# The beginning of a 256-token, four-layer network on one core: the first norm's weights spread by transposes, the first tile's squares and scaling split over two engines

## Chip, cores and metric

The kernel runs on one core of a Trainium2 chip. The metric is the device time of one execution in microseconds; the figure of a kernel is the median of its runs. One execution is also recorded by the hardware profiler, and all times "from the span's start" below are from that record. The engines are TensorE (PE, with its weight loads PEld), VectorE (DVE), ScalarE (ACT), GpSimd (POOL) and SyncE (SP), which here only issues DMAs.

## What is computed

Four layers over x of shape (1, 256, 1024): stick-breaking attention with a gated convolution MLP, forgetting attention with another, a pooling layer and a latent attention layer. What matters here is the very first step, the RMS norm of x with the weights `sb_pre_g`, and the projection to values that follows it:

```python
def rmsnorm(x, g):
    xf = x.astype(jnp.float32)
    y = xf * lax.rsqrt(jnp.mean(xf * xf, axis=-1, keepdims=True) + RMS_EPS)
    return (y * g.astype(jnp.float32)).astype(x.dtype)
...
a = rmsnorm(h, sb_pre_g[layer])
q, k, v = jnp.split(a @ sb_w_qkv[layer], 3, axis=-1)
```

## The kernel before

**Tiling.** The 256 tokens are two tiles of 128 (i = 0 and 1), one token a partition; `h[:, i, :]` holds the 1024 features of a token. A norm works on that layout: the squares of a row are summed (`square`, ACT, two halves of 512 features, `HALF`), POOL makes the reciprocal root (`rstd_of`: two adds and a power), and `scaled` multiplies h by it and by the norm's weights on DVE, in two halves, into a tile `a`. The weights have to stand in all 128 partitions for this; `gain` (L301) loads them with a DMA that reads the same 4 KB row for each partition, 512 KB in all.

**Transposes.** The matmuls need features on the partitions. `transpose_split` (L341) lets TensorE transpose four 128x128 blocks of `a` into one PSUM tile `psT`, then splits the result into two fp32r numbers: `hi_copy` (L55, ACT) rounds it, `lo_sub` (L59, DVE) takes the rest. `aT[n]` holds features 512n to 512n+511; `all_T` does both n.

**Weights.** Each weight chunk is loaded into `raw` by SP (`load_w`, L141, ring of three), and split in parts the same way, `wh` on ACT and `wl` on DVE (`bg_hi`, `bg_lo`; `bg(m)` puts m parts into the engines' queues). The first two chunks come in eight parts of one block of 128 features by 512 columns each; with the sixth part's DMA the second token tile of x is loaded (L150). A product is three matmuls (L78, L79, L81): high by high, high by low, low by high.

**Order.** Nothing is scheduled by a planner: each engine works off its queue in the order in which the code is written, and waits by semaphores for the others. At the beginning (L565 to L584) that is: 24 transposes of the identity on TensorE into a tile `warm` that nobody reads, the norm of token tile 0 (`a0`), `bg(2)` for weight parts 0 and 1, `all_T(a0)`, `bg(4)`, the squares of tile 1, `bg(2)`, the scaling of tile 1 (`a1`), then `values_all`, whose first group of matmuls (n = 0, i = 0) reads `aT` of tile 0; `all_T(a1)` stands behind this group and ahead of the second one (n = 0, i = 1).

SP's queue at the beginning: both halves of tile 0 of x, the norm's weights, six weight parts, tile 1 of x, two more weight parts, and then whole chunks.

PSUM: two pools of four tiles (2 KB a partition), `pacc` (accumulators) and `pmm` (short-lived results).

Of the kernel before, what the change touches and what calls it, by code (L numbers as in the profile page):

```python
# [7 lines left out]
F32 = mybir.dt.float32  # L8
# [3 lines left out]
AF = mybir.ActivationFunctionType  # L12
ALU = mybir.AluOpType
PSUM = bass.MemoryType.PSUM

P = 128
S = 256
NT = S // P
D = 1024
KD = D // P  # L20
# [4 lines left out]
EPS = 1e-6  # L25
# [10 lines left out]
def tile_net(ctx: ExitStack, tc: tile.TileContext, t, out):  # L36
    nc = tc.nc
    ctx.enter_context(tc.manual_schedule())
    pe, act, dve, pool = nc.tensor, nc.scalar, nc.vector, nc.gpsimd
# [6 lines left out]
    nat = ctx.enter_context(tc.tile_pool(name="nat", bufs=2))  # L46
    jk = ctx.enter_context(tc.tile_pool(name="jk", bufs=1))
    sm = ctx.enter_context(tc.tile_pool(name="sm", bufs=4))
# [15 lines left out]
    def split(hi, lo, src, scale=None):  # L64

        hi_copy(hi, src, 1.0 if scale is None else scale)
        lo_sub(lo, src, hi, scale)
# [15 lines left out]
    def acc_tile(name):  # L83
        return pacc.tile([P, 512], F32, tag="acc", name=name)
# [4 lines left out]
    def mm_tile(name):  # L89
        return pmm.tile([P, 512], F32, tag="mm", name=name)  # L90

    def tok(i):
        return slice(i * P, (i + 1) * P)
# [11 lines left out]
    def table_set(i):  # L105
        act.add_instruction(mybir.InstLoadActFuncSet(
            act_func_set_id=i, name=nc.get_next_instruction_name()))
# [33 lines left out]
    def load_w(upto):  # L141
        while nxt["load"] <= min(upto, len(specs) - 1):
            v = specs[nxt["load"]][0]
            raw = rawp.tile([P, RAWW], F32, tag="raw", name="raw")
            rv = raw[:, :v.shape[1] * v.shape[2]].rearrange("p (a b) -> p a b", a=v.shape[1])

            for q in specs[nxt["load"]][1] if nxt["load"] < 2 else ():
                k0, k1 = parts[q]["cut"][0:2]
                nc.sync.dma_start(out=rv[:, k0:k1], in_=v[:, k0:k1])
                if q == 5:  # L150
                    load_x(1)
            if nxt["load"] >= 2:
                nc.sync.dma_start(out=rv, in_=v)
            loaded[nxt["load"]] = rv
            nxt["load"] += 1

    def bg_hi():

        n = nxt["hi"]
        if n >= len(parts) or (n >= WBUFS and parts[n - WBUFS]["used"] < parts[n - WBUFS]["need"]):  # L160
            return False
        q = parts[n]
        load_w(q["chunk"])
        k0, k1, c0, c1 = q["cut"]
        for nm, pl_ in (("wh", whp), ("wl", wlp)):
            w = pl_.tile([P, TW], F32R, tag=nm, name=nm)
            q[nm] = w[:, :q["n"]].rearrange("p (a b) -> p a b", a=k1 - k0)
        q["raw"] = loaded[q["chunk"]][:, k0:k1, c0:c1]
        hi_copy(q["wh"], q["raw"], q["scale"] or 1.0)
        nxt["hi"] += 1  # L170
        return True

    def bg_lo():
        while nxt["lo"] < nxt["hi"]:
            n = nxt["lo"]
            q = parts[n]
            lo_sub(q["wl"], q.pop("raw"), q["wh"], q["scale"])
            nxt["lo"] += 1
            if n == specs[q["chunk"]][1][-1]:
                load_w(q["chunk"] + RAWB)  # L180

    def bg(m=1):
        for _ in range(m):
            bg_lo()
            if not bg_hi():
                break
        bg_lo()
# [104 lines left out]
    h = cst.tile([P, NT, D], F32, name="h")  # L292

    def load_x(i):
        for n in range(2):
            s_ = slice(512 * n, 512 * n + 512)
            nc.sync.dma_start(out=h[:, i, s_], in_=t["x"][0, tok(i), s_])

    load_x(0)

    def gain(name, idx=None, g=None):  # L301
        src = t[name][idx] if idx is not None else t[name]
        n = src.shape[0]
        if g is None:
            g = gp.tile([P, D], F32, tag="g", name="g")[:, 0:n]
        nc.sync.dma_start(out=g, in_=src.unsqueeze(0).to_broadcast([P, n]))
        return g

    g_pre = gain("sb_pre_g", 0)
    load_w(RAWB - 1)  # L310


    ident = cst.tile([P, P], F32, name="ident")
# [3 lines left out]
    epsc = cst.tile([P, 2], F32, name="epsc")  # L317
# [7 lines left out]
    def mean_sq(srcs, n):  # L325

        ss = sm.tile([P, 2], F32, tag="ss", name="ss")
        for j, x in enumerate(srcs):
            square(x, n, ss[:, j:j + 1])
        return ss[:, 0:len(srcs)]  # L330

    def rstd_of(ss, tag="rstd"):
        r = sm.tile([P, 1], F32, tag=tag, name="rstd")
        s0 = ss[:, 0:1]
        pool.tensor_tensor(out=s0, in0=s0, in1=epsc[:, 0:1], op=ALU.add)  # L335
        if ss.shape[1] == 2:
            pool.tensor_tensor(out=s0, in0=s0, in1=ss[:, 1:2], op=ALU.add)
        pool.tensor_tensor(out=r, in0=s0, in1=epsc[:, 1:2], op=ALU.pow)
        return r

    def transpose_split(src, dst, i, b, m=4):  # L341

        ps = mm_tile("psT")
        for j in range(m):
            pe.transpose(ps[:, tok(j)], src[:, tok(b + j)], ident)  # L345
        split(dst[0][:, 0:m, tok(i)], dst[1][:, 0:m, tok(i)],
              ps[:, 0:m * P].rearrange("p (k c) -> p k c", k=m))

    def all_T(src, dst, i):
        for n in range(2):  # L350
            transpose_split(src, dst[n], i, 4 * n)

    HALF = [slice(n * 512, (n + 1) * 512) for n in range(2)]

    def scaled(i, r, g):

        a = nat.tile([P, D], F32, tag="a", name="a")
        for s_ in HALF:
            dve.scalar_tensor_tensor(out=a[:, s_], in0=h[:, i, s_], scalar=r, in1=g[:, s_],
                                     op0=ALU.mult, op1=ALU.mult)  # L360
        return a
# [7 lines left out]
    def square(x, n, ss):  # L369

        junk = jk.tile([P, 512], BF16, tag="junk", name="junk")
        act.activation(out=junk[:, 0:x.shape[1]], in_=x, func=AF.Square, scale=float(n) ** -0.5,  # L372
                       accum_out=ss)
# [28 lines left out]
    def new_aT():  # L402
        return [tuple(atp.tile([P, KD // 2, S], F32R, tag=f"aT{x}{n}", name="aT") for x in "hl")
                for n in range(2)]
# [62 lines left out]
    def edge(tail0, tail1, acc, add, g, dst):  # L467


        tail0()  # L470
        half, fin = add(0, acc[0])
        half(0)
        half(1)
        bg_hi()
        fin()
        r0 = norm_r(0)
        tail1()
        half, fin = add(1, acc[1])
        half(0)
        a0 = scaled(0, r0, g)  # L480
        half(1)
        all_T(a0, dst, 0)
        bg_hi()
        fin()
        r1 = norm_r(1)
        return scaled(1, r1, g), (r0, r1)
# [78 lines left out]
    K8 = [(k, k) for k in range(KD)]  # L565
    aT = new_aT()
    table_set(NLE_SET)
    warm = mm_tile("warm")
    for _ in range(24):
        pe.transpose(warm[:, 0:P], ident, ident)  # L570
    a0 = scaled(0, rstd_of(mean_sq([h[:, 0, s_] for s_ in HALF], D)), g_pre)
    bg(2)
    all_T(a0, aT, 0)
    bg(4)
    ss1 = mean_sq([h[:, 1, s_] for s_ in HALF], D)
    bg(2)
    a1 = scaled(1, rstd_of(ss1, "rn"), g_pre)
    bg(0)
    with tc.tile_pool(name="sb", bufs=2) as sb, tc.tile_pool(name="sbv", bufs=1) as sbv:
        vv = [sbv.tile([P, NT, D], F32R, name=n) for n in ("vh", "vl")]  # L580
# [95 lines left out]
        with tc.tile_pool(name="ld", bufs=1) as ld:  # L676
            a1 = attention(s0, s1, s2, s3, post, W["sb_o"], oT, g_post, aT2,
                           lambda: load_params(ld), lambda: gain("ffn_pre_g", 0), mm_tile)
        aT = aT2
# [113 lines left out]
    with tc.tile_pool(name="fxa", bufs=1) as fxa:  # L793
# [3 lines left out]
        a1, rn = ffn(0, aT, a1, lambda: (gain("ffn_post_g", 0), gain("kv_norm_g")), sT)  # L797
# [3 lines left out]
        with tc.tile_pool(name="fx", bufs=2) as fx, tc.tile_pool(name="fxv", bufs=1) as fxv:  # L801
# [26 lines left out]
            for b in (0, 32, 64, 96):  # L828
# [16 lines left out]
                                     op1=ALU.subtract)  # L845
            pool.memset(fe, 1.0)
            dve.tensor_tensor_scan(out=fc, data0=fe, data1=fy, initial=0.0, op0=ALU.mult,
                                   op1=ALU.add)
# [45 lines left out]
            def f3(p):  # L894
                heads_out(p, vv, st.pop(("p", p)), oT)

            aT = new_aT()
            a1 = attention(f0, f1, f2, f3, lambda p: bg(1), W["fx_o"], oT, g_post, aT,
                                     gates_T, lambda: gain("ffn_pre_g", 1), acc_tile)

    pT = new_aT()
    a1 = ffn(1, aT, a1, lambda: (gain("ffn_post_g", 1), gain("pool_norm_2", 0)), pT)[0]
    aT = pT


    with tc.tile_pool(name="pl", bufs=2) as pl_, tc.tile_pool(name="plc", bufs=1) as plc:
# [95 lines left out]
        g_pre = gain("mla_norm_2", 0)  # L1002
# [28 lines left out]
        def lat_mm(x, i, k0, k1):  # L1031
            n, w = lat_w[x]
            if k0 == 0:
# [5 lines left out]
        a1 = edge(lambda: out_rows(acc[0], 0, st["y", 3], wo, k4, False, True, by_half=True),  # L1039
                  lambda: out_rows(acc[1], 1, st["y", 3], wo, k4, False, True, by_half=True),  # L1040
                  acc, plain_add, g_pre, mT)[0]
        aT = mT
# [407 lines left out]
```

## Time and profile before

| | |
|---|---|
| median of 3 runs | 996.11 us (993.27, 996.11, 997.5) |
| profiled execution, its own time | 995.02 us |
| its span, first to last instruction | 992.6 us |
| mean granted TensorE clock | 0.997 |
| TensorE busy | 977.5 us (98%) |
| DVE, ACT, POOL busy | 754.3, 608.4, 72.4 us |
| DMA traffic over the span | 171 GB/s read |

A row of the timeline has the start and the length in us, the engine, the line of the kernel, the operation, what it writes and reads, a count where equal instructions were merged, and in brackets the idle time of the engine ahead of it with what ended it. The chain of waits is followed back from the last instruction: at each step to what released it. Rows that group instructions have busy us, mean ns of one, and the idle time ahead. A matmul's length contains the pipeline behind it, so that matmuls in a row overlap: their pace is read from the starts, or from the chain.

### The profile page before, as it was taken

To read this page: it belongs to the slowest core of one execution; us is meant where nothing else is said; L and a number is where in the kernel's file an instruction comes from. 1 tells how busy PE (TensorE), PEld (TensorE's weight loads), DVE (VectorE), ACT (ScalarE), POOL (GpSimd) and SP (SyncE) were. 2 spreads that over 40 slices of the span, in tenths; PEclk is the share of its full clock that TensorE was granted. 3 is DMA by queue.
4 is the path that set the end of the run, shared out by engine and by line. 5 is a ranking of instruction groups with operands and counts; after the bars stand their busy time and mean duration, and the time that the engine had idled before them with its cause. 6 is when DMAs were issued, how large, how long until landed. Compare 5 with 4: busy or idle time off the path is not lost.

```text
span 992.6 us, 17595 instructions
## 1 busy us (share of the span) xinstructions
PE 977.5 (98%) x6955; PEld 900.3 (91%) x6955; DVE 754.3 (76%) x1299; ACT 608.4 (61%) x1050; POOL 72.4 (7%) x182
## 2 busy tenths in 40 slices
PE   8999999999999999999999999999999999999997
PEld 6999789999887799879999988899999899999996
DVE  6577788899845879977999954777757677886876
ACT  6489867677634657666667643565535455766663
POOL 1022220000001100020000000200000020110100
PEclk9999999999999999999999999999999999999999
DMA  8824346575652654435665665275555344544421
GB/s 300 258 87 148 128 152 212 163 243 191 249 193 85 197 188 149 151 105 170 208 203 184 212 241 184 68 253 207 178 208 191 109 133 134 202 156 138 160 100 42
DMA packets 116292, 170.79 MB, mean 172 GB/s; under 512 B 4226, under 2 KB 93682, under 8 KB 116210
## 3 DMA queue, kind: packets, MB, share of 16 engines
q1 hardware_dynamic: 116146, 169.68, 51.6%
q8 instruction: 54, 0.88, 0.4%
q14 instruction: 28, 0.23, 0.1%
q0 software_dynamic: 64, 0.00, 0.0%
HBM read 168.62 MB, written 1.05 MB: 171 GB/s over the span
## 4 chain that ended last, share of the span: by engine, by line
PE 92%; DVE 3%; ACT 2%; DMA 1%; issue 1%; POOL 1%; SPq 0%; POOLq 0%; DVEq 0%; ACTq 0%
PE psu L70 10%; PE psu L71 10%; PE psu L72 10%; PE accD L71 4%; PE accD L72 4%; PE accD L70 4%; PE psq L70 4%; PE psq L72 4%; PE psq L71 4%; PE accO L70 3%; PE accO L72 3%; PE accO L71 2%; PE accP L71 2%; PE accP L72 2%; PE accP L70 2%; PE psT L345 1%
## 5 line engine op out<-in xcount | busy, mean ns | idle before, releaser
L59 DVE TENSOR_TENSOR wl<-raw,wh 128x1024 fp32r<-128x1024 f32 (+3 forms) x300 | 352.6, 1196 | 102.6 <-ACT wh L55 99.6
L55 ACT ACTIVATE wh<-raw 128x1024 fp32r<-128x1024 f32 (+3 forms) x316 | 315.5, 1026 | 98.9 <-PE accD L72 44.8
L70 PE MATMUL psu<-aT,wh 128*128 128x256 f32 x864 | 241.3, 279 | 0.0
L71 PE MATMUL psu<-aT,wh 128*128 128x256 f32 x864 | 240.6, 278 | 0.0
L72 PE MATMUL psu<-aT,wl 128*128 128x256 f32 x864 | 240.4, 278 | 0.0
L70 PEld LDWEIGHTS psu<-aT,wh 128*128 128x128 f32 x864 | 162.2, 188 | 0.0
L72 PEld LDWEIGHTS psu<-aT,wl 128*128 128x128 f32 x864 | 162.2, 188 | 0.0
L71 PEld LDWEIGHTS psu<-aT,wh 128*128 128x128 f32 x864 | 161.9, 187 | 0.0
L703 DVE SCALAR_TENSOR_TENSOR yc<-psu,conv,yc 128x255 f32<-128x255 f32 (+1 forms) x160 | 73.3, 479 | 7.7 <-ACT yc L696 4.7
L70 PE MATMUL accD<-wh,gh 128*128 128x512 f32 x176 | 69.3, 394 | 0.0
L71 PE MATMUL accD<-wl,gh 128*128 128x512 f32 x176 | 69.3, 394 | 0.0
L72 PE MATMUL accD<-wh,gl 128*128 128x512 f32 x176 | 69.3, 394 | 0.0
L335 POOL TENSOR_TENSOR ss<-ss,epsc 128x1 f32<-128x1 f32 x24 | 11.7, 488 | 625.5 <-ACT junk L372 625.4
L70 PE MATMUL psq<-aT,wh 128*128 128x256 f32 x192 | 54.1, 282 | 0.1
L72 PE MATMUL psq<-aT,wl 128*128 128x256 f32 x192 | 53.5, 279 | 0.0
L71 PE MATMUL psq<-aT,wh 128*128 128x256 f32 x192 | 53.5, 279 | 0.0
L708 ACT ACTIVATE yc<-yc 128x256 f32<-128x256 f32 x44 | 18.4, 418 | 54.2 <-DVE yc L703 54.2
L696 ACT ACTIVATE yc<-psu,conv 128x256 f32<-128x256 f32 x80 | 40.5, 556 | 8.2 <-PE psu L72 8.2
L72 PEld LDWEIGHTS accD<-wh,gl 128*128 128x128 f32 x176 | 32.9, 187 | 8.1
L70 PEld LDWEIGHTS accD<-wh,gh 128*128 128x128 f32 x176 | 32.9, 187 | 8.1
L71 PEld LDWEIGHTS accD<-wl,gh 128*128 128x128 f32 x176 | 32.9, 187 | 8.1
L55 ACT ACTIVATE qkh<-psq 128x512 fp32r<-128x512 f32 x32 | 19.0, 594 | 31.9 <-PE psq L72 31.6
(334 smaller groups left out, 2276.0 us busy)
## 6 DMA issues: line engine op xcount, KB each, us to landing
raw<-in_w_up_dram SPq DMA_DIRECT2D x44, 1024.0 KB, 5.1
raw<-in_w_down_dram SPq DMA_DIRECT2D x22, 1024.0 KB, 4.9
raw<-in_pool_w_in_dram SPq DMA_DIRECT2D x16, 1024.0 KB, 7.6
raw<-in_sb_w_qkv_dram SPq DMA_DIRECT2D x10, 1024.0 KB, 6.2
raw<-in_w_kvf_dram SPq DMA_DIRECT2D x8, 1024.0 KB, 5.6
raw<-in_pool_w_out_dram SPq DMA_DIRECT2D x8, 1024.0 KB, 5.2
raw<-in_mla_w_in_dram SPq DMA_DIRECT2D x8, 1024.0 KB, 5.5
raw<-in_mla_w_out_dram SPq DMA_DIRECT2D x8, 1024.0 KB, 6.4
```

Of the source, the lines that this page charges most:

```text
L55: act.activation(out=hi, in_=src, func=AF.Copy, scale=scale)
L59: (eng or dve).tensor_tensor(out=lo, in0=src, in1=hi.bitcast(F32), op=ALU.subtract)
L70: pe.matmul(ps, lhsT=l[0], rhs=r[0], start=first, stop=False)
L71: pe.matmul(ps, lhsT=l[0], rhs=r[1], start=False, stop=False)
L72: pe.matmul(ps, lhsT=l[1], rhs=r[0], start=False, stop=last)
L335: pool.tensor_tensor(out=s0, in0=s0, in1=epsc[:, 0:1], op=ALU.add)
L345: pe.transpose(ps[:, tok(j)], src[:, tok(b + j)], ident)
L696: act.activation(out=y[:, u, :], in_=ps[:, u * S:(u + 1) * S], func=AF.Identity, bias=cp[:, 132 + q:133 + q], scale=cp[:, 88 + q:89 + q])
L703: dve.scalar_tensor_tensor(out=y[:, u, d:S], in0=ps[:, u * S:(u + 1) * S - d], scalar=w, in1=y[:, u, d:S], op0=ALU.mult, op1=ALU.add)
L708: act.activation(out=y[:, 0, :], in_=y[:, 0, :], func=AF.Gelu_apprx_tanh)
```

## The change

1. `g_pre = gain(...)`, the 512 KB DMA on SP, is gone. Instead ACT issues, ahead of its table load, a DMA of the 1024 weights as 8 rows of 128 (`g_row`, 4 KB).
2. TensorE transposes `g_row` into PSUM (`gT_ps`), DVE copies the result to `g_col` (128 partitions, 8 columns), and TensorE transposes each column, repeated 128 times by a step of zero, into `g_ps`, two PSUM tiles of 128x512 in which each partition holds the weights. Blocks 4 to 7 come first. Around these stand 7, 3 and 4 transposes of the identity in place of the 24.
3. The squares of tile 0: ACT takes half 0, DVE half 1 (`tensor_tensor_reduce`, with the division by 1024 and EPS folded in; so POOL's add of EPS is gone).
4. The scaling of tile 0: half 0 in one DVE instruction as before; half 1 is multiplied by the weights on DVE (`y0`) ahead of the reciprocal root, and by that root on ACT.
5. Weight part 0 is split ahead of `aT[0]` and part 1 ahead of `aT[1]`, instead of both ahead of both.
6. Tile 1 is scaled by the weights out of PSUM.

```diff
+    g_row = sm.tile([KD, P], F32, tag="grow", name="g_row", bufs=1)
+    act.dma_start(out=g_row, in_=t["sb_pre_g"][0].rearrange("(k p) -> k p", p=P))
     load_x(0)
...
-    g_pre = gain("sb_pre_g", 0)
     load_w(RAWB - 1)
...
-    warm = mm_tile("warm")
-    for _ in range(24):
-        pe.transpose(warm[:, 0:P], ident, ident)
-    a0 = scaled(0, rstd_of(mean_sq([h[:, 0, s_] for s_ in HALF], D)), g_pre)
-    bg(2)
-    all_T(a0, aT, 0)
+    warm = acc_tile("warm")
+
+    def busy(n):
+        for _ in range(n):
+            pe.transpose(warm[:, 0:P], ident, ident)
+
+    busy(7)
+    gT_ps = acc_tile("gT_ps")
+    pe.transpose(gT_ps[:, 0:KD], g_row, ident[0:KD, 0:KD])
+    g_col = sm.tile([P, KD], F32, tag="gcol", name="g_col", bufs=1)
+    dve.tensor_copy(g_col, gT_ps[:, 0:KD])
+    busy(3)
+    g_ps = [mm_tile("g_ps") for n in range(2)]
+    for k in (4, 5, 6, 7, 0, 1, 2, 3):
+        pe.transpose(g_ps[k // 4][:, tok(k % 4)], g_col[:, k:k + 1].to_broadcast([P, P]), ident)
+    busy(4)
+
+    ss0 = sm.tile([P, 2], F32, tag="ss", name="ss")
+    square(h[:, 0, HALF[0]], D, ss0[:, 0:1])
+    a0 = nat.tile([P, D], F32, tag="a", name="a")
+    y0 = nat.tile([P, D], F32, tag="a", name="y0")
+    dve.tensor_tensor_reduce(out=y0[:, HALF[0]], in0=h[:, 0, HALF[1]], in1=h[:, 0, HALF[1]],
+                             scale=1.0 / D, scalar=EPS, op0=ALU.mult, op1=ALU.add,
+                             accum_out=ss0[:, 1:2])
+    dve.tensor_tensor(out=y0[:, HALF[1]], in0=h[:, 0, HALF[1]], in1=g_ps[1], op=ALU.mult)
+    r0 = sm.tile([P, 1], F32, tag="rstd", name="rstd")
+    pool.tensor_tensor(out=ss0[:, 0:1], in0=ss0[:, 0:1], in1=ss0[:, 1:2], op=ALU.add)
+    pool.tensor_tensor(out=r0, in0=ss0[:, 0:1], in1=epsc[:, 1:2], op=ALU.pow)
+    act.activation(out=a0[:, HALF[1]], in_=y0[:, HALF[1]], func=AF.Copy, scale=r0)
+    dve.scalar_tensor_tensor(out=a0[:, HALF[0]], in0=h[:, 0, HALF[0]], scalar=r0, in1=g_ps[0],
+                             op0=ALU.mult, op1=ALU.mult)
+    for n in range(2):
+        bg(1)
+        transpose_split(a0, aT[n], 0, 4 * n)
     bg(4)
     ss1 = mean_sq([h[:, 1, s_] for s_ in HALF], D)
     bg(2)
-    a1 = scaled(1, rstd_of(ss1, "rn"), g_pre)
+    r1 = rstd_of(ss1, "rn")
+    a1 = nat.tile([P, D], F32, tag="a", name="a")
+    for n, s_ in enumerate(HALF):
+        dve.scalar_tensor_tensor(out=a1[:, s_], in0=h[:, 1, s_], scalar=r1, in1=g_ps[n],
+                                 op0=ALU.mult, op1=ALU.mult)
```

The order on ACT from the start of the program to the last part of the first two chunks: before,

```order
L106 ACT_TABLE_LOAD
L372 ACTIVATE junk,ss<-h 128x512 x2
L55 ACTIVATE wh<-raw 128x512 x2
L55 ACTIVATE aT<-psT 128x4x128 x2
L55 ACTIVATE wh<-raw 128x512 x4
L372 ACTIVATE junk,ss<-h 128x512 x2
L55 ACTIVATE wh<-raw 128x512 x2
```

and now (line numbers are those of the changed kernel):

```order
L301 DMA g_row<-in_sb_pre_g_dram 8x128
L106 ACT_TABLE_LOAD
L374 ACTIVATE junk,ss<-h 128x512
L598 ACTIVATE a<-y_160,rstd 128x512
L55 ACTIVATE wh<-raw 128x512
L55 ACTIVATE aT<-psT 128x4x128
L55 ACTIVATE wh<-raw 128x512
L55 ACTIVATE aT<-psT 128x4x128
L55 ACTIVATE wh<-raw 128x512 x4
L374 ACTIVATE junk,ss<-h 128x512 x2
L55 ACTIVATE wh<-raw 128x512 x2
```

One of the two squares of tile 0 has gone to DVE, half of the scaling has come in its place, and the first two parts and the two halves of `aT` alternate.

On DVE, the same place of the program, as a difference (ISA is the multiply with a sum, and the read of that sum):

```order
-L359 SCALAR_TENSOR_TENSOR a<-h,rstd,g 128x512 x2
-L59 TENSOR_TENSOR wl<-raw,wh 128x512 x2
-L59 TENSOR_TENSOR aT<-psT,aT 128x4x128 x2
+L1480 UNCONDITIONAL_BRANCH
+L580 COPY g_col<-gT_ps 128x8
+L591 ISA y_160,ss<-h 128x512
+L591 ISA ss 128x1
+L594 TENSOR_TENSOR y_160<-h,g_ps 128x512
+L599 SCALAR_TENSOR_TENSOR a<-h,rstd,g_ps 128x512
+L59 TENSOR_TENSOR wl<-raw,wh 128x512
+L59 TENSOR_TENSOR aT<-psT,aT 128x4x128
```

DVE had nothing to do ahead of the scaling; now a copy that waits for TensorE, a square and a multiply stand there, and one half of the scaling is left.

On TensorE, ahead of the first matmul with weights:

```order
-L570 MATMUL warm<-ident 128x128 x24
-L345 MATMUL psT<-ident,a 128x128 x8
+L1480 UNCONDITIONAL_BRANCH
+L574 MATMUL warm<-ident 128x128 x7
+L578 MATMUL gT_ps<-ident,g_row 128x8
+L574 MATMUL warm<-ident 128x128 x3
+L584 MATMUL g_ps<-ident,g_col 128x128 x8
+L574 MATMUL warm<-ident 128x128 x4
+L347 MATMUL psT<-ident,a 128x128 x8
```

The transposes for the weights stand between those of the identity, the first behind a DMA and the eight behind DVE's copy.

On SP one row is gone, the DMA of the norm's weights between x and the first weight part; all its other rows stand in the order of before.

## The prediction

> **What bounds the kernel now.** I read the page first, then the span in two stretches, then the chain of waits and the timeline of the first 18 us.
>
> The page: the span, TensorE's share, and the shares of the chain that ended last.
>
> ```profile
> span 992.6 us, 17595 instructions
> PE 977.5 (98%) x6955; PEld 900.3 (91%) x6955; DVE 754.3 (76%) x1299; ACT 608.4 (61%) x1050; POOL 72.4 (7%) x182
> ...
> PE 92%; DVE 3%; ACT 2%; DMA 1%; issue 1%; POOL 1%; SPq 0%; POOLq 0%; DVEq 0%; ACTq 0%
> ```
>
> Two stretches, cut where the second group of value matmuls starts (stretch, length, busy time of PE, PEld, DVE, ACT and POOL with counts, granted clock, DMA share, GB/s).
>
> ```profile
> 0.00:18.10 18.10, 14.16 (x64) 11.24 (x64) 8.98 (x14) 10.13 (x20) 3.07 (x15) 0.91 0.89 317
> 18.10:992.60 974.50, 963.37 (x6891) 889.04 (x6891) 745.32 (x1285) 598.29 (x1030) 69.29 (x167) 1.00 0.51 169
> ```
>
> Behind 18.1 us TensorE works 963.4 of 974.5 us, and the change touches nothing there. Ahead of it 3.9 us are idle, and much of the 14.2 "busy" is warm-up or the modelled ends of matmuls that wait. The whole change lives in these 18.1 us, under 2% of the time: it can neither save nor lose much.
>
> The chain of waits in them (start, length, what):
>
> ```profile
> 1.72 5.44 DMA g<-in_sb_pre_g_dram
> ...
> 7.29 0.76 DVE a L359
> ...
> 8.09 1.98 PE psT L345 x8
> ...
> 10.10 0.60 ACT aT L55
> 10.70 1.61 ACT wh L55 x4
> ...
> 14.70 0.70 DVE wl L59
> ...
> 15.44 0.50 PE accV L79
> ...
> 17.46 0.63 PE psT L345 x4
> ...
> 18.13 0.50 PE accV L78
> ```
>
> The norm's weights, spread by one DMA, arrive at 7.2 us and release the scaling of the first token tile; its transposes follow, and from 10.1 us ACT sets the pace (rounding of aT and of eight weight parts). The timeline shows how near the next two limits stand:
>
> ```profile
> 1.72 0.42 SPq L306 DMA_DIRECT2D g<-in_sb_pre_g_dram  x1
> 2.18 3.25 SPq L149 DMA_DIRECT2D raw<-in_sb_w_qkv_dram  x6
> 3.50 0.63 ACT L372 ACTIVATE junk<-h 128x512 bf16<-128x512 f32 x1 [1.41 <-DMA h<-in_x_dram]
> 4.03 0.19 ACT L372 ACTIVATION_READ_ACCUMULATOR junk<-h 128x1 f32 x1
> 4.25 0.63 ACT L372 ACTIVATE junk<-h 128x512 bf16<-128x512 f32 x1
> 4.37 0.19 POOL L335 TENSOR_TENSOR ss<-ss,epsc 128x1 f32<-128x1 f32 x1 [2.91 <-ACT junk L372]
> 4.79 0.19 ACT L372 ACTIVATION_READ_ACCUMULATOR junk<-h 128x1 f32 x1
> 5.12 0.19 POOL L337 TENSOR_TENSOR ss<-ss 128x1 f32<-128x1 f32 x1 [0.55 <-ACT junk L372]
> 5.39 0.55 POOL L338 TENSOR_TENSOR rstd<-ss,epsc 128x1 f32<-128x1 f32 x1
> ...
> 8.25 1.29 ACT L55 ACTIVATE wh<-raw 128x512 fp32r<-128x512 f32 x2 [3.27 <-DMA raw<-in_sb_w_qkv_dram]
> ```
>
> rstd is there at 5.94, so 1.35 us ahead of its use; the first weight part lands at 8.25, after 3.27 us of an idle ACT. Taking the weights' DMA away alone moves the scaling to 5.94; what it gives then depends on when the first part of raw lands.
>
> **The change part by part.**
>
> *Squares shared.* ACT squares half 0 as before, from 3.50 to 4.22. DVE squares half 1 when that half lands: no row shows the landing, but it lies between 3.93 (half 0's plus 0.43, half of what the two issues take) and 4.25 (the second square starts there without waiting). I take 4.1. Its length, and other lengths that I need:
>
> ```profile
> L763 DVE CUSTOM_DVE_ANT_0 pt<-z,gm 128x256 f32<-128x256 f32 x2 | 0.8, 420 | 0.0
> ...
> L763 DVE CUSTOM_DVE_ANT_0 pt<-z,gm 128x128 f32<-128x128 f32 x2 | 0.6, 286 | 0.0
> ...
> L763 DVE DVE_READ_ACCUMULATOR2_ANT mx<- 128x1 f32 x4 | 0.3, 84 | 0.0
> ```
>
> ```profile
> L59 DVE TENSOR_TENSOR wl<-raw,wh 128x512 fp32r<-128x512 f32 x8 | 5.1, 687 | 1.0 <-ACT wh L55 1.0
> L55 ACT ACTIVATE wh<-raw 128x512 fp32r<-128x512 f32 x8 | 4.6, 622 | 3.3 <-DMA raw<-in_sb_w_qkv_dram 3.3
> ...
> L386 DVE TENSOR_TENSOR y<-accO,g 128x512 f32<-128x512 f32 x2 | 1.3, 686 | 0.0
> ...
> L562 DVE COPY pscale<-psc 128x16 f32<-128x16 f32 x1 | 0.2, 163 | 0.0
> ```
>
> The same form costs 286 ns for 128 elements and 420 for 256, so about 0.69 us for 512, plus 0.08 for the read: done at 4.87. POOL before started 0.14 after the last read (4.98 to 5.12) and needed 0.82 for add and power: 0.96. So r0 stands at 5.83 (bounds 5.66 to 5.98) against 5.94. **Worth 0.1 us**, no more; the add of eps that goes (L335) was beside ACT's second square.
>
> *Scaling shared.* DVE multiplies half 1 by the gains (0.69, 4.87 to 5.56) while POOL works, so it costs nothing; if the gains were late it would stand ahead of everything else on DVE. Then DVE scales half 0 (0.76 as before) and ACT half 1, both from 5.9. The ACT copy with a scale per row isn't there at this width; the plain copy of 512 takes 0.62, DVE's scaling 0.76, and I take 0.75. Both halves are done at 6.65; before, the first alone was done at 8.05. Gains read from PSUM cost DVE nothing more: 686 ns with accO from PSUM, 687 without. So a1's scaling from PSUM, later, stays as it was.
>
> *Gains spread by TensorE.* g_row is 4 KB in 8 rows, issued by ACT ahead of its table load at about 0.8 us; the load, now some 0.4 later, still ends ahead of 3.50. After the landing T come one transpose (a half-clock transpose in flight takes about 0.4), a copy (0.16) and hand-offs (0.1): T + 0.65. Then four transposes, at half clock 0.99 (half of the chain's 1.98 for eight), give g_ps[1] at T + 1.65 and g_ps[0] at T + 2.65. Against the need at 4.87 and 5.9 that is free up to T = 3.2. x's first 256 KB landed 2.7 us after their issue (0.81 to 3.50); 4 KB issued at the same time should be no later: T is 2.5 to 3.5, and I take 3.0. At 3.5 it costs 0.3.
>
> *What goes from the DMAs.* 512 KB leave the queue between x and the weights, and SP issues raw 0.46 earlier (1.72 instead of 2.18). The traffic while they moved:
>
> ```profile
> 4.00:5.00 1.00, 1.00 (x9) 1.00 (x8) 0.00 (x0) 0.94 (x4) 0.19 (x1) 1.00 0.98 256
> 5.00:6.00 1.00, 0.75 (x7) 0.51 (x5) 0.00 (x0) 0.00 (x0) 0.74 (x2) 1.00 0.57 158
> ...
> 7.00:8.00 1.00, 0.00 (x0) 0.00 (x0) 0.71 (x2) 0.00 (x0) 0.00 (x0) 0.96 1.04 395
> ```
>
> 0.52 MB at 395 GB/s are 1.3 us, at 256 GB/s 2.0. The first part of raw lands at 6.2 to 6.9 instead of 8.25; I take 6.6. The far bound is the earlier issue alone, 7.8: that would be so if the poor stretch (57% busy, 158 GB/s) belongs to the beginning of the weights' own packets.
>
> *ACT's new order.* With 0.60 to 0.62 each: scaled half 1 until 6.65, wh0 until 7.3; the first four transposes start at 6.7 and take 0.63 at full clock, so aT0 runs 7.4 to 8.0, wh1 to 8.6, aT1 to 9.2. The four parts wh2 to wh5 then start at **9.2 instead of 10.70**, 1.5 us earlier. With half clock the four take 0.99, and they start at 9.55: 1.15 earlier. From there ACT, DVE and TensorE have the order of before: wh2 to wh5, two squares, wh6 and wh7, DVE's wl7, the last value matmuls, a1's transposes. The transfers stay ahead, being 1.6 earlier themselves. All of 18.13 moves by that.
>
> The transposes of the warm-up (23 instead of 24, now with gaps) keep the clock up or don't:
>
> ```profile
> 2.40:4.40 2.00, 2.00 (x11) 2.00 (x10) 0.00 (x0) 0.87 (x3) 0.03 (x1) 1.00 1.04 339
> 4.60:5.60 1.00, 1.00 (x11) 0.91 (x9) 0.00 (x0) 0.38 (x2) 0.40 (x2) 1.00 0.72 193
> 8.09:10.09 2.00, 1.98 (x9) 1.59 (x9) 1.79 (x3) 1.75 (x3) 0.00 (x0) 0.50 1.05 403
> ```
>
> Eleven transposes took 2.0 us, then eleven 1.0 us: the pace doubled after 3 us of transposes alone (the clock column has no lower entry that early). After 2.35 us without work (5.75 to 8.09) it was halved again. In the new program the gap ahead of a0's transposes is about 1 us shorter, so I reckon with full clock. The Trainium skill, "TensorE: Matmul & The Clock Gate", Part 4, says that full clock doesn't engage for transposes, which don't count as work in the same way; the doubled pace here speaks against it, and by it a0's transposes would run at half clock and the gain be 1.15.
>
> **Sum**: squares 0.1, scaling no longer behind the weights' DMA 1.3, its transposes sooner and ACT's order about even: 1.5 at full clock, 1.15 at half, and I take **1.4 us**. Nothing behind 18.1 gives it back: loads there hang on DVE's releases and move with them. The profiled execution took 995.02 (span 992.6 and 2.4 around it), which gives 993.6; the runs' median is 996.11, 1.1 higher, which gives 994.7. The time to come is a median of runs as well, so I put it halfway: **994.2**.
>
> **The rivals.**
> - *Half clock at a0's transposes*: 1.15 gained, 994.5. For it: TensorE idles around 5 to 6.7, and has short gaps while it waits for g_row and g_col; against: before, 2.35 us without work stood ahead of the half clock. The rule of the Trainium skill above, were it so here, would lead to this case.
> - *The weights stay late* (raw at 7.8): wh0, aT0, wh1, aT1 follow each other from 7.8 to 10.2, and wh2 gains 0.5: 995.1. The slack stretch at 5 to 6 us speaks for it, the 0.52 MB taken away against it.
> - *g_row late, slower than before.* Place: TensorE's one transpose of g_row, on which DVE waits ahead of its square. By the steps above wh2 starts at T + 6.2 at half clock; it breaks even with 10.70 at T = 4.5. A small transfer behind weights does take that long:
>
> ```profile
> lp<-in_pool_scale_dram SPq DMA_DIRECT2D x1, 8.0 KB, 4.6
> ```
>
>   4.6 after 0.8 is T = 5.4, 0.9 us slower: 996.5. Against it: it starts together with x, with nothing ahead of it.
> - *The lead is lost*: TensorE arrives earlier and waits for later weights: 995.6, no change. The traffic at 25 to 40 us is dense, but TensorE didn't wait there.
>
> **How the numbers follow.** Forecast 0.45, half clock 0.25, late weights 0.15, late g_row 0.1, lead lost 0.05. The three runs spread from 993.27 to 997.5, 2 us to either side, more than the cases differ. Range 991.8 to 996.8: the forecast less 2.4 and just over the late g_row's 996.5. The bound of what can be told from no change, 0.5%, is 5 us; no case reaches it, since only 3.9 us of TensorE's idle time stand in the stretch at all. Faster by over that 0.04, within 0.93, slower 0.03, for the spread alone.
>
> **What would show it.** Right: DVE's scaling of half 0 starts near 5.9, ACT's first wh near 6.7 behind its own scaling and no longer behind a DMA, aT0 near 7.4, the four wh near 9.2, the second group of value matmuls near 16.7 instead of 18.13. Wrong: ACT still waits for raw (late weights); DVE's first copy after 3.9 (late g_row); eight transposes of a0 in 1.7 us or more (half clock); the 16.7 reached but a wait for weights before 60 us (lead lost).

## The result, and the profile after

The changed kernel takes **1007.07 us** (median of five, 1006.71 to 1007.88) against 996.11: 1.0116 times as long, interval 1.0097 to 1.0134. One run of the kernel before, of 2470.69 us, is left out of the ratio. Some 11 us slower, where 2 us faster had been forecast, and 10 us above the forecast range. The profiled execution took 1007.07, its span is 1005.3.

The beginning is not where they went. The same two stretches as before, cut where the second group of value matmuls starts:

```profile
0.00:16.60 16.60, 13.87 (x63) 9.91 (x63) 9.91 (x17) 9.90 (x19) 3.04 (x14) 1.00 0.91 320
16.60:1005.30 988.70, 978.22 (x6891) 905.37 (x6891) 745.69 (x1285) 599.46 (x1030) 68.93 (x167) 1.00 0.50 167
```

The second group starts at 16.6 instead of 18.1, as forecast. The rest, 6891 matmuls in both, takes 988.7 us instead of 974.5: **14.2 us more, in which TensorE is busy**, at a clock of 1.00. No wait was added: TensorE's idle time in this stretch is 10.5 us, and was 11.1. The timeline of the beginning, against the steps of the prediction:

```profile
3.12 0.27 PE L578 MATMUL gT_ps<-ident,g_row 8*128 8x8 f32 x1
...
4.39 0.69 DVE L591 CUSTOM_DVE_ANT_0 y<-h 128x512 f32<-128x512 f32 x1 [0.79 <-DMA h<-in_x_dram]
...
5.11 0.69 DVE L594 TENSOR_TENSOR y<-h,g_ps 128x512 f32<-128x512 f32 x1
...
5.51 0.55 POOL L597 TENSOR_TENSOR rstd<-ss,epsc 128x1 f32<-128x1 f32 x1
...
6.10 0.72 ACT L598 ACTIVATE a<-y,rstd 128x512 f32<-128x512 f32 x1 [1.78 <-POOL rstd L597]
6.10 0.75 DVE L599 SCALAR_TENSOR_TENSOR a<-h,rstd,g_ps 128x512 f32<-128x512 f32 x1 [0.30 <-POOL rstd L597]
6.73 0.61 ACT L55 ACTIVATE wh<-raw 128x512 fp32r<-128x512 f32 x1
...
9.09 2.19 ACT L55 ACTIVATE wh<-raw 128x512 fp32r<-128x512 f32 x4
```

The square on DVE, the multiply under POOL's work, the root at 6.06, both halves of the scaling at once, the first weight part right behind, the four parts at 9.09: each within 0.3 us of its forecast. Where the later time goes, the pages of the two kernels show in the line of the commonest matmul. Before:

```profile
PE 977.5 (98%) x6955; PEld 900.3 (91%) x6955; DVE 754.3 (76%) x1299; ACT 608.4 (61%) x1050; POOL 72.4 (7%) x182
...
L70 PE MATMUL psu<-aT,wh 128*128 128x256 f32 x864 | 241.3, 279 | 0.0
```

And after:

```profile
PE 992.1 (99%) x6954; PEld 915.3 (91%) x6954; DVE 755.6 (75%) x1302; ACT 609.4 (61%) x1049; POOL 72.0 (7%) x181
...
L70 PE MATMUL psu<-aT,wh 128*128 128x256 f32 x864 | 244.1, 283 | 0.0
```

TensorE is busy for 14.6 us more with the same matmuls (and one transpose less), DVE and ACT for 1.3 and 1.0 us. A matmul's 279 or 283 ns contain its pipeline, so the pace shows better in how many start in a fixed stretch. Two stretches of the first MLP, in the middle of the long loop over `psu` (columns as before). Before:

```profile
144.00:184.00 40.00, 40.00 (x355) 40.00 (x354) 34.85 (x54) 28.05 (x43) 0.00 (x0) 1.00 0.68 219
200.00:250.00 50.00, 50.00 (x427) 50.00 (x426) 47.38 (x80) 35.64 (x60) 0.00 (x0) 1.00 0.64 213
```

After:

```profile
144.00:184.00 40.00, 40.00 (x336) 40.00 (x335) 33.06 (x52) 27.03 (x41) 0.00 (x0) 1.00 0.64 208
200.00:250.00 50.00, 50.00 (x419) 50.00 (x418) 46.51 (x79) 35.01 (x58) 0.00 (x0) 1.00 0.65 214
```

In the first, a matmul every 112.7 ns before (40/355) and every 119.0 after; in the second 117.1 and 119.3. Nothing of the program's code differs there. What differs is where the operands lie. The built programs place their SBUF tiles at these bytes of a partition:

```
            before     after
wh (first)   52320     52320
wl (first)   85088     85088
g_row            -    139360   (512 bytes)
g_col            -    139872   (32 bytes)
aT (first)  140192    140736
gh          162720    163264
```

`g_row` has 8 partitions of data but takes its 512 bytes from all, and `g_col` 32 more; both are in the pool `sm`, which stands ahead of `aT`. So aT and all behind it moved by 544 bytes, wh and wl did not. The theories:

- **A, placement**: the matmuls read weights and activations at addresses whose distance changed, and that makes their pace.
- **B, the start**: the new beginning (other PSUM tiles, other phase) sets TensorE into a slower rhythm that lasts.

### The profile page after: what moved, and what is told of

It reads as the page before. It is cut to its first block, busy times and chain, and to the rows that moved or that the text cites. A ratio compares the mean times of both kernels' runs of the same rounds, so it can differ in the third digit from the quotient of the medians.

```text
span 1005.3 us, 17593 instructions
## 1 busy us (share of the span) xinstructions
PE 992.1 (99%) x6954; PEld 915.3 (91%) x6954; DVE 755.6 (75%) x1302; ACT 609.4 (61%) x1049; POOL 72.0 (7%) x181
## 4 chain that ended last, share of the span: by engine, by line
PE 94%; DVE 2%; ACT 1%; POOL 1%; issue 1%; DMA 0%; POOLq 0%; SPq 0%; DVEq 0%; ACTq 0%
PE psu L70 10%; PE psu L72 10%; PE psu L71 10%; PE psq L70 4%; PE accD L71 4%; PE accD L72 4%; PE accD L70 4%; PE psq L72 4%; PE psq L71 4%; PE accO L70 3%; PE accO L72 3%; PE accO L71 3%; PE accP L71 1%; PE accP L70 1%; PE accP L72 1%; PE accV L79 1%
## 5 line engine op out<-in xcount | busy, mean ns | idle before, releaser
L70 PE MATMUL psu<-aT,wh 128*128 128x256 f32 x864 | 244.1, 283 | 0.0
L72 PE MATMUL psu<-aT,wl 128*128 128x256 f32 x864 | 243.8, 282 | 0.0
L71 PE MATMUL psu<-aT,wh 128*128 128x256 f32 x864 | 243.3, 282 | 0.0
L71 PEld LDWEIGHTS psu<-aT,wh 128*128 128x128 f32 x864 | 163.1, 189 | 0.0
L70 PEld LDWEIGHTS psu<-aT,wh 128*128 128x128 f32 x864 | 162.6, 188 | 0.0
L72 PEld LDWEIGHTS psu<-aT,wl 128*128 128x128 f32 x864 | 162.4, 188 | 0.0
L71 PE MATMUL accD<-wl,gh 128*128 128x512 f32 x176 | 69.8, 397 | 0.0
L70 PE MATMUL accD<-wh,gh 128*128 128x512 f32 x176 | 69.8, 396 | 0.0
L72 PE MATMUL accD<-wh,gl 128*128 128x512 f32 x176 | 69.8, 396 | 0.0
L70 PE MATMUL psq<-aT,wh 128*128 128x256 f32 x192 | 54.8, 285 | 0.1
L72 PE MATMUL psq<-aT,wl 128*128 128x256 f32 x192 | 54.2, 282 | 0.0
L71 PE MATMUL psq<-aT,wh 128*128 128x256 f32 x192 | 53.9, 281 | 0.0
L72 PEld LDWEIGHTS accD<-wh,gl 128*128 128x128 f32 x176 | 33.1, 188 | 8.1
L70 PEld LDWEIGHTS accD<-wh,gh 128*128 128x128 f32 x176 | 33.2, 188 | 8.0
L71 PEld LDWEIGHTS accD<-wl,gh 128*128 128x128 f32 x176 | 33.1, 188 | 8.0
```

The lines of the kernel that those rows point to most:

```text
L70: pe.matmul(ps, lhsT=l[0], rhs=r[0], start=first, stop=False)
L71: pe.matmul(ps, lhsT=l[0], rhs=r[1], start=False, stop=False)
L72: pe.matmul(ps, lhsT=l[1], rhs=r[0], start=False, stop=last)
```

## The experiments

Times are medians, with the ratio to the kernel before in runs on the same chip. "Pace" is the mean distance between the starts of neighbouring `psu` matmuls over the trace, in ns: 116.8 before, 120.2 after.

**e1, the kernel before with the 544 bytes alone.**

```diff
+    pad = sm.tile([P, 128], F32, tag="grow", name="pad", bufs=1)
+    pad2 = sm.tile([P, KD], F32, tag="gcol", name="pad2", bufs=1)
```

> The kernel before, its code unchanged, with two unused SBUF tiles (512 and 32 bytes a partition) where the change puts g_row and g_col, so that aT and all tiles behind it stand 544 bytes later, as in the changed kernel; wh and wl stay. Theory A (placement: TensorE reads aT and the like at other addresses, and its matmuls follow each other more slowly): about 1007 us to 1009 us, psu matmuls 120 ns apart instead of 113 to 118. Theory B (the pace is set by how TensorE starts, or by which PSUM tiles it begins with; not by addresses in SBUF): 996 us, pace as before.

Measured: 1010.45 us, ratio 1.0138 (1.0122 to 1.0153), pace 120.2.

**e2, the change without the 544 bytes.**

```diff
-    g_row = sm.tile([KD, P], F32, tag="grow", name="g_row", bufs=1)
+    g_row = cosT.rearrange("p a b -> p (a b)")[0:KD, :]
...
-    g_col = sm.tile([P, KD], F32, tag="gcol", name="g_col", bufs=1)
+    g_col = sinT[:, 0, 0:KD]
```

> The changed kernel with g_row and g_col put into the space of cosT and sinT (written only much later), so that every SBUF tile stands where it stood before the change; queues, PSUM tiles and order are the changed kernel's. Theory A: 1.4 us under the kernel before, about 994.6, pace of psu 113 to 118 ns. Theory B: stays at 1007.

Measured: 991.15 us, ratio 0.9939 (0.9925 to 0.9954), pace 116.3. The same stretches of e1:

```profile
144.00:184.00 40.00, 40.00 (x336) 40.00 (x335) 33.22 (x50) 26.61 (x41) 0.00 (x0) 1.00 0.63 204
200.00:250.00 50.00, 50.00 (x420) 50.00 (x419) 46.97 (x79) 35.24 (x59) 0.00 (x0) 1.00 0.64 211
```

and of e2:

```profile
144.00:184.00 40.00, 40.00 (x355) 40.00 (x354) 35.16 (x56) 27.85 (x44) 0.00 (x0) 1.00 0.69 222
200.00:250.00 50.00, 50.00 (x427) 50.00 (x426) 47.49 (x79) 34.89 (x60) 0.00 (x0) 1.00 0.63 212
```

e1 has the counts of the changed kernel to one matmul, e2 those of the kernel before. B is out: e2 has the changed start, with its PSUM tiles and queues, and keeps the fast pace. The unused bytes alone make the loss. (Not quite all tiles of e2 stand where they stood: the tiles `gm` and `gates` of the later layers take another buffer of their rings, 4096 bytes on, as they do in the changed kernel.) That e2 is 6 us under the kernel before, rather than 1.4, is more than the beginning gives; that is taken up below.

**e3 and e4, which property of the place.** e3 puts 32 more bytes behind g_row, 576 in all; e4 puts 544 bytes at the front of all tiles of the kernel before.

```diff
+    pad = sm.tile([P, 8], F32, tag="pad", name="pad", bufs=1)
...
+    pad = cst.tile([P, 136], F32, name="pad")
```

> The changed kernel with 32 more unused bytes behind g_row: aT and what follows stand 576 bytes later than before the change, so at 32 bytes past a multiple of 64 as before, and as wh and wl do. Theory A in the form 'half of a 64-byte line': about 995. Theory A in a coarser form (which of larger blocks): stays near 1007. Theory B: 1007.

Measured: 1000.92 us, ratio 1.0039 (1.0024 to 1.0053), pace 119.2. The simple form, half of a 64-byte line, doesn't hold: better than 544, but not at 995.

> The kernel before with 544 unused bytes at the very front of its SBUF tiles: wh, wl, aT and all else move together, and keep their distances. Theory A if the distance of weights and activations counts: 996. Theory A if the place of aT by itself counts (start within 64 bytes): about 1007. Theory B: 996.

Measured: 997.13 us against 997.11, ratio 1.0004 (0.9990 to 1.0017). Moved together by this shift, the tiles cost nothing (pace 117.7 in the one trace). It is the **distance**, not the place.

**e5, the distance of which tiles.** The 544 bytes behind aT instead of ahead of it:

```diff
     aT = new_aT()
+    pad = atp.tile([P, 136], F32, tag="pad", name="pad")
```

> The changed kernel at the old places (as e2), with 544 unused bytes behind aT: aT stands where it stood, all tiles behind it (qkh, yc, gh, gl and so on) 544 bytes later. If the distance of aT to wh and wl is what counts (psu, psq, accS, psz read just these): near e2, 991 to 993, psu about 116.5 ns apart. If the tiles behind aT count (results of ACT and DVE, gh and gl): about 1004, psu about 120 ns.

Measured: 994.92 us, ratio 1.0004 (0.9994 to 1.0013). psu keeps its pace, 116.5, though the tiles that ACT and DVE write beside it (yc, gh, gl) have moved. The expected 991 to 993 is missed by 2 us: matmuls that read tiles behind aT slow down, accD (gh, gl) from 233.3 to 234.3 ns and psq from 118.3 to 120.4 in the mean. The loop over psq between 346 and 405 us has both kinds side by side: pairs that read aT start 116.9 ns apart, pairs that read fT, a tile behind aT, 119.8. In e2 it is 116.7 and 116.6, in the changed kernel 119.9 for both. So a tile that keeps its distance keeps the pace, and one that moves loses it, in the same loop of one run. (The first loop over psq, which reads aT alone, goes from 115.6 to 117.8 as well; that is the mixture of two paces of the last section.) Most of the loss, but not all, sits between aT and the weights.

**e6 to e10, e13 and e14, the distance varied.** All are e2 with `pad` of so many bytes in `sm`, ahead of aT.

> As e2, aT and all behind it 32 bytes later. Fine form (the place within 64 bytes, against that of wh and wl): slow, 1003 to 1006, since 544 is 32 more than a multiple of 64. Coarse form (steps of 512, the step of the weights' blocks): near 991.

> As e2, aT and all behind it 64 bytes later. Fine form: near 991. Coarse form: near 991 as well; but e3 (576 = 512 + 64) was at 1000.9, so either the 512 or the 64 costs some 9 us: slow here (1000) means the 64 does it.

> As e2, aT and all behind it 512 bytes later. Fine form: near 991. Coarse form: slow, 1000 to 1005.

> As e2, aT and all behind it 128 bytes later. So far: 0 and 512 bytes fast (psu about 116.4 ns apart), 32 slowest (120.2), 64 in between (119.2). If the pattern repeats after 128 bytes: about 991, psu 116.4. If only after 512: some other pace, 995 to 1007.

> As e2, 96 bytes later. If the place within 64 bytes decides the slowest pace: as with 32, about 1007, psu 120.2. If each step of 32 has a pace of its own: anything between 991 and 1007.

> As e2, aT and all behind it 256 bytes later. So far (bytes later: us): 0: 991.2, 32: 1007.3, 64: 1000.7, 96: 998.2, 128: 984.0, 512: 991.4. If places repeat after 256 bytes: 991, psu about 116.4 ns apart. If after 128 with one odd value: 984. If only after 512: anything up to 1007.

> As e2, 384 bytes later (256 more than e9). If places repeat after 256 bytes: as e9, 984, accD about 229 ns apart. If not: 991 or another value.

Measured, with the changed kernel and e3 in their places:

| bytes | run | us | ratio to before (interval) | pace of psu |
|---|---|---|---|---|
| 0 | e2 | 991.15 | 0.9939 (0.9925 to 0.9954) | 116.3 |
| 32 | e6 | 1007.34 | 1.0130 (1.0115 to 1.0146) | 120.2 |
| 64 | e7 | 1000.70 | 1.0062 (1.0046 to 1.0079) | 119.2 |
| 96 | e10 | 998.20 | 1.0020 (0.9997 to 1.0043) | 117.7 |
| 128 | e9 | 983.97 | 0.9896 (0.9835 to 0.9956) | 115.0 |
| 256 | e13 | 992.00 | 0.9963 (0.9946 to 0.9981) | 118.1 |
| 384 | e14 | 985.43 | 0.9899 (0.9874 to 0.9924) | 115.2 |
| 512 | e8 | 991.37 | 0.9967 (0.9956 to 0.9979) | 116.4 |
| 544 | the change | 1007.07 | 1.0116 (1.0097 to 1.0134) | 120.2 |
| 576 | e3 | 1000.92 | 1.0039 (1.0024 to 1.0053) | 119.2 |

The runs were taken on several chips, on which the medians of the kernel before lie between 994.96 and 997.11. Times repeat after 256 bytes as far as tried (0, 256 and 512; 128 and 384; 32 and 544; 64 and 576); the paces are each from one trace, and e13's is of its slowest run, 995.34. 32 and 544 are the worst, 128 and 384 the best. My rules set up beforehand were too simple: the fine form foresaw e6's loss but not e7's, e9 lies below both of its forecasts, and in e14 accD has not the 229 ns of e9, as expected, but 233.3. The change at the old places with 128 more bytes, e9, is the fastest of all, 1% under the kernel before (0.4 to 1.7% by the interval).

**e15, the distance without the change.** The kernel before with `pad` of 128 bytes in `sm`.

> The kernel before, with 128 unused bytes ahead of aT and nothing else changed. If the distance alone makes e9's time, independent of the change: 1.4 to 3 us over e9, 985.5 to 987, about 1% under the kernel before. If e9's time needs the changed beginning: 993 to 997.

Measured: 988.92 us, ratio 0.9932 (0.9908 to 0.9956): two thirds of e9's gain come with the bytes alone, by the medians; the two intervals touch. It lies 2 us over what was expected.

**e16, which reads meet.** Of the operands of psu, wl alone gets another distance: 32 bytes ahead of it, and 480 in `sm`, so that aT moves by 512, which in e8 changed nothing.

```diff
+    wlpad = wlp.tile([P, 8], F32, tag="pad", name="wlpad", bufs=1)
...
+    pad = sm.tile([P, 120], F32, tag="pad", name="pad", bufs=1)
```

> As e2, with wl alone at 32 bytes more in its distance: wl stands 32 bytes later, aT and all behind it 512 (which changed nothing in e8). If what counts is the pair of reads of TensorE itself (the weights being loaded against the operand streamed at the same time), only the loads of wl, one in three, are disturbed: psu between 116.4 and 120.2 ns, about 117.5, and the disturbed interval is that of L71, during which wl is loaded for L72; time 994 to 998. If aT's own place, or its distance to wh alone, counts: 991, as e2 and e8.

Measured: 997.54 us, ratio 1.0019 (1.0008 to 1.0031), pace 118.2. All ten runs (996.89 to 998.01) lie above all ten of e13 on the same chip (990.07 to 995.34), so the place of wl costs time by itself (the tiles of the norms behind wl move by 32 bytes too, but psu doesn't read them). The pace lies between e2 and e6 as the theory of the two reads wanted it, but so does e13's (118.1). The stretches:

```profile
144.00:184.00 40.00, 40.00 (x343) 40.00 (x342) 33.97 (x53) 26.94 (x42) 0.00 (x0) 1.00 0.64 206
200.00:250.00 50.00, 50.00 (x427) 50.00 (x426) 47.50 (x80) 35.68 (x60) 0.00 (x0) 1.00 0.64 213
```

But the interval that I named was wrong, and the mean pace comes about in another way. Between 200 and 240 us the starts of L70 and L71 lie 117.4 ns apart, those of L71 and L72 116.7, those of L72 and the next L70 119.3; in e2 they are 117.8, 117.4 and 118.1. The three together are 353.4 and 353.3 ns, so that here e16 isn't slower at all. It is slower in the first stretch, 116.6 against 112.7: e16 keeps a pace near 118 through its whole trace, where e2 runs near 113 for a part of the time. That one load in three is disturbed is therefore not shown.

That it is TensorE's own two reads, weights and streamed operand, fits e4, e5 and e16; how they meet is not shown. A rival is that DVE and ACT, which read and write beside these reads, stand in the way. The traces speak against it: the starts of psu in the changed kernel lie 119.9 ns apart while DVE doesn't work, 120.1 while ACT doesn't, 119.9 while neither does and 120.2 while both do (116.8, 117.0, 117.6 and 116.7 before).

**e11 and e12, the parts of the change at the beginning**, both at the old places; the diffs show lines added to the changed kernel. e11 keeps only the gains spread by transposes; squares and scaling of tile 0 are done as before the change. e12 lets ACT round weight part 0 ahead of its half of the scaling.

```diff
+    r0 = rstd_of(mean_sq([h[:, 0, s_] for s_ in HALF], D))
...
+        dve.scalar_tensor_tensor(out=a0[:, s_], in0=h[:, 0, s_], scalar=r0, in1=g_ps[n],
+                                 op0=ALU.mult, op1=ALU.mult)
+    bg(2)
+    all_T(a0, aT, 0)
```

> Old places. Of the change only the gains spread by transposes (with their g_row and g_col and the warm-up around them); squares of tile 0 both on ACT, its scaling both halves on DVE, weight parts 0 and 1 ahead of both halves of aT, as before the change. By the steps of the prediction the root is there at about 5.95, DVE scales 6.0 to 7.45, aT0 from 7.5, the four wh start at about 9.0 and the second group of value matmuls at 16.7 to 17.1, against 17.0 in e2: the sharing of squares and scaling is worth under 0.3 us. If the sharing is what brings the lead: second group at 17.7 or later.

```diff
+    bg_hi()
     act.activation(out=a0[:, HALF[1]], in_=y0[:, HALF[1]], func=AF.Copy, scale=r0)
...
+    bg(1)
+    all_T(a0, aT, 0)
```

> Old places. The changed kernel, with ACT rounding weight part 0 ahead of its half of the scaling, and part 1 ahead of both halves of aT: ACT idled for 1.78 us there while the first part of raw had landed by about 5.7. Expected: first wh near 5.7, the four wh at 8.8 instead of 9.1, second group some 0.3 us earlier; in total 990.8 to 991.2, not to be told from e2 by its time.

Measured: 992.63 (0.9971, 0.9946 to 0.9996) and 992.17 us (0.9965, 0.9942 to 0.9988), not told apart from each other; what counts is the timeline. e11:

```profile
6.39 1.41 DVE L589 SCALAR_TENSOR_TENSOR a<-h,rstd,g_ps 128x512 f32<-128x512 f32 x2 [2.80 <-POOL rstd L339]
6.59 1.26 ACT L55 ACTIVATE wh<-raw 128x512 fp32r<-128x512 f32 x2 [1.21 <-DMA raw<-in_sb_w_qkv_dram]
...
9.04 0.62 ACT L55 ACTIVATE wh<-raw 128x512 fp32r<-128x512 f32 x1
```

and e12:

```profile
6.70 0.64 ACT L55 ACTIVATE wh<-raw 128x512 fp32r<-128x512 f32 x1 [2.60 <-DMA raw<-in_sb_w_qkv_dram]
...
7.24 0.71 ACT L598 ACTIVATE a<-y,rstd 128x512 f32<-128x512 f32 x1
```

e11 starts its third weight part at 9.04 and its second group at 16.59, the changed kernel at 9.09 and 16.63. Sharing squares and scaling brings nothing that these traces show: in the twelve traces that have the changed beginning, the second group starts between 16.25 and 17.02. The lead comes from the small DMA of the gains. e12 shows why its own idea fails: the first part of raw lands at 6.7, so ACT's 1.78 us of idle time could not be filled; its second group starts at 16.9, within that spread. The 5.7 was read from SP's issues, which don't show a landing.

## Why the prediction was wrong

*The beginning* was right in its steps. Root at 6.06 (5.83 forecast, and just past the bound of 5.98; the second half of x landed later, 4.39 for 4.1), gains free up to T = 3.2 (the transpose of g_row started at 3.12, behind an idle time of 0.33), raw at 6.6 (6.70 in e12), four parts at 9.2 (9.09), second group at 16.7 (16.63). The chain of waits after has the steps in the forecast order:

```profile
6.10 0.76 DVE a L599
...
6.90 0.67 PE psT L347 x4
...
7.60 0.60 ACT aT L55
...
8.83 0.69 DVE wl L59
...
9.57 0.51 PE accV L79
```

Four transposes in 0.67 us are full clock, as forecast. e2, with the same queues, had the half-clock rival's case instead: its four took from 6.84 to 7.96, and its second group came at 17.0, where that rival would have it (18.13 less 1.15). Not for the rival's reason, an idle TensorE, though: the four transposes of the identity just ahead took 1.06 us there against 0.60 in the changed kernel, so the pace had not doubled yet.

```profile
6.84 1.52 PE L346 MATMUL psT<-ident,a 128*128 128x128 f32 x8
...
7.96 0.60 ACT L55 ACTIVATE aT<-psT 128x512 fp32r<-128x512 f32 x1 [0.83 <-PE psT L346]
```

The Trainium skill's rule that the prediction weighed there ("TensorE: Matmul & The Clock Gate", Part 4, transposes don't bring full clock) doesn't hold in the changed kernel: nothing but transposes had run when a0's four took 0.67 us, and the starts of the transposes go from 213 to 110 ns apart at 5.4 us. (In the kernel before they go from 213 to 109 at 4.5 us; the prediction's eleven in 2.0 us count those that reach into the stretch.)

*The step that failed* is the first one: "The whole change lives in these 18.1 us", "the change touches nothing there", and after the sum "Nothing behind 18.1 gives it back". I compared the queues, the waits and the order, found them equal behind the beginning, and took equal instructions for equal times. Two new tiles, together 544 bytes, in a pool ahead of aT don't show in an order of instructions; they show in the addresses. e1 has the loss from the 544 bytes alone (13 us), e2 the change without it (6 us faster than before, not 11 slower). No rival had this mechanism, and the bound "since only 3.9 us of TensorE's idle time stand in the stretch at all" counted idle time alone, as if a busy TensorE could not get slower.

*The sizes*: the beginning gave 1.5 us where 1.4 had been taken. That the two agree so well is in part luck. In the four traces that have the beginning of before, the second group starts at 17.70 (e4), 18.13 (before), 19.18 (e15) and 19.49 (e1), since the DMAs land at other times: the norm's weights at 7.16 before and at 8.18 in e15. In the mean of the traces the beginnings are 18.6 and 16.6, 2.0 us apart. The loss behind it is 14.2 us in the profiled execution: 2592 psu matmuls at 3.4 ns (120.2 less 116.8) make 8.8 of it, 986 psq intervals at 3.0 ns (121.7 less 118.7) another 3.0; the other matmuls have the rest.

*The parts of the change*: "Worth 0.1 us, no more" for the shared squares is not contradicted (e11 shows no gain from the sharing, and could not show so small a one). The 1.3 us for "scaling no longer behind the weights' DMA" is the lead, and e11 has it without the sharing.

*What stays open*: how the two reads meet, so that 32 bytes more are bad and 128 good; and why e2 is 6 us under the kernel before, when its beginning gives 1.1 in its trace, or 2.0 by the means. A part may be told by the next section: at a good distance the pace itself has two values.

## What to carry to other kernels

A tile that is added to a pool moves all pools behind it. Where TensorE is the bound, compare the addresses of weights and streamed operands in the two built programs before saying that the rest is untouched, and put small temporaries where they move nothing (into a tile that is written later, or behind all operands of matmuls; e5 shows that behind aT alone isn't far enough). And try the distance for its own sake: 128 unused bytes with nothing else changed were worth 0.7% here (e15, 6 us), some four times what the whole change at the beginning was meant to bring.

## What the runs showed of the hardware that was not expected

**The distance of weights and streamed operand in SBUF sets the pace of fp32r matmuls**: 115.0 to 120.2 ns for 256 columns, over distances that differ by 32 to 576 bytes, with the same instructions and no wait. These are means over a trace; next comes what they are made of. The Trainium skill, "TensorE: Matmul & The Clock Gate", Part 2, says that TensorE reads weights and streamed operand through two ports, so that loading the next weights takes no read bandwidth from the running matmul. If the two reads are what meets here, e1 and e4 differ from that: 544 bytes between the two cost 13 us, 544 bytes ahead of both cost nothing.

**One distance can have two paces.** In the kernel before, the first stretch above runs at 112.7 ns a matmul and the second at 117.1, with the same tiles. The switch comes in the trace at 182 us, where four transposes stand between two groups of psu; on either side the distances of the starts repeat unchanged (113, 113, 114 and then 117, 118, 118). In e9 it is the other way round:

```profile
144.00:184.00 40.00, 40.00 (x343) 40.00 (x342) 34.15 (x54) 26.61 (x43) 0.00 (x0) 1.00 0.65 209
200.00:250.00 50.00, 50.00 (x443) 50.00 (x442) 47.64 (x81) 35.82 (x61) 0.00 (x0) 1.00 0.64 211
```

116.6 ns and then 112.9. There too the switch comes at the four transposes. So it is not the tiles of one loop that are fast; such a short interruption can go along with a change from one rhythm to the other. At 32, 64, 96, 544 and 576 bytes, and in e16, no twelve psu matmuls in a row average under 116.5 ns. At the multiples of 128 bytes nearly all stand at one of the two paces, and the share of the faster one differs: 70% in e9, 66% in e14, 51% in e11, 47% in e15, 37% in e2, 35% in e8, 26% before, 24% in e12, 13% in e4 and none in e13. So for psu the means at these distances are mixtures of the same two rhythms, and 128 and 384 bytes are better there by a larger share of the faster one; what decides the share is open. e2 and the kernel before have equal counts in the two stretches above, but not in the second MLP. Before:

```profile
500.00:560.00 60.00, 60.00 (x512) 60.00 (x511) 55.91 (x97) 41.94 (x72) 0.00 (x0) 1.00 0.62 206
```

e2:

```profile
500.00:560.00 60.00, 60.00 (x519) 60.00 (x518) 56.24 (x96) 43.00 (x73) 0.00 (x0) 1.00 0.60 198
```

Seven matmuls more in 60 us, 0.8 us in this stretch alone. This would also fit that the kernel before spreads over 990.4 to 1001.3 us in 25 runs on one chip, and the changed kernel, whose pace in the two stretches is 119.0 and 119.3, over 1006.7 to 1007.9 in five; that the rhythms make this spread was not tested.
